# A two-block mixer network: the modulation's weights loaded as tiles of four k blocks, and its column-packed products issued in fours

## The chip, the cores and the metric

The kernel runs on one core of one Trainium2 chip. The metric is the device time of one execution in microseconds; lower is better. TensorE (PE) does the matrix products, VectorE (DVE), ScalarE (ACT) and GpSimd (POOL) the elementwise work, and SyncE (SP) issues nearly all loads, in the order of its queue. Each engine works through its own instructions strictly in program order.

## The reference, cut to what matters

Two blocks, each of two layers, work on 256 context and 256 latent tokens of 1024 features, all in float32. Each layer begins with a modulation: a vector `c` (one for the latent tokens, one for the context) goes through silu and a large matrix, and its result is cut into shifts, scales and gates.

```python
def first_block(x, c, ctx, c_ctx, ada_w, ada_b, ...):
    s_lat = jax.nn.silu(c)
    s_ctx = jax.nn.silu(c_ctx)
    for i in range(DEPTH):                      # DEPTH = 2, ada_w[i] is 1024 x 6144
        m_l = jnp.split((s_lat @ ada_w[i] + ada_b[i])[:, None, :], 6, axis=-1)
        m_c = jnp.split(s_ctx @ ada_w[i] + ada_b[i], 6, axis=-1)
        ul = snake(modulate(hl, m_l[0], m_l[1]))
        ...                                     # i = 0: GLA mixer, i = 1: SSD mixer
        hl = layer_norm(DEEPNORM_ALPHA * hl + m_l[2] * snake(yl), ...)
        hl = layer_norm(DEEPNORM_ALPHA * hl + m_l[5] * sq_relu_mlp(modulate(hl, m_l[3], m_l[4]), ...), ...)
...
def second_block(x, c, ctx, c_ctx, norm_g, w_ada, b_ada, w_in, ...):
    for l in range(DEPTH):                      # w_ada[l] is 1024 x 3072
        shift, scale, gate = jnp.split(jax.nn.silu(c) @ w_ada[l] + b_ada[l], 3, axis=-1)
        shift_c, scale_c, gate_c = jnp.split(jax.nn.silu(c_ctx) @ w_ada[l] + b_ada[l], 3, axis=-1)
        ...                                     # three attentions, gated and merged
```

The change touches only how `silu(c) @ ada_w` and `silu(c) @ w_ada` are computed.

## The kernel before, in words

**The program** runs through stages, with approximate times of the profile: the modulation of the first layer that must be there first (0 to 31 us), the GLA mixer (31 to 345), its output projection and norm (345 to 450), the first feed-forward net, called ffn0 (450 to 835), the SSD mixer (835 to 1190), its end and the start of the next stage (1190 to 1290), then the second feed-forward net, and from 1620 us the second block. The large projections all go through `gemm` (products at L432): a weight unit of two k blocks (512 KB, tile `wr`, three buffers) is loaded by SP at L380, split into a high part `wh` by ACT (L385) and a low part `wl` by DVE or POOL (L390), two buffers each, and multiplied in three terms per k block.

**The modulation** is cut into chunks of 512 columns, each 1024 x 512 values, that is eight k blocks of 128 rows. The first four chunks are computed at once (`early`, tile `wst`). The other 32 wait in a background queue (`self.bg`): after each weight unit, `gemm` calls `tick`, which adds `self.rate` to an account and records further steps of the queue while the account is positive; a step says what it costs. `finish(n)` records steps until n chunks are left. So the background work is woven into the projections by a rate: `FRATE` in ffn0, `SRATE` in the SSD mixer, `GRATE` in the GLA mixer. After that a scheduler orders each engine's instructions by a simulated timeline, and `not_before` keeps a load from going ahead of the products recorded before it.

A chunk is one generator, `ada_chunk`. There are two kinds:

- **22 of the 32 background chunks have two vectors** (`c` and `c_ctx`). Their k blocks are loaded one by one (256 KB each, tile `wrd`, four buffers), and each is the moving operand of one float32 product with 32 stationary columns (L531): 512 columns stream through a quarter of PE's columns. Products g = 0..3 write to rows 32g of one bank, so each has its own quarter of the array. A chunk has eight such products. A float32 product shows as two records in the profile. The four rows of sums are then added by four small products with `sel` (L540), once per group of up to four chunks, after a copy by ACT (L537).
- **10 of the 32 have one vector.** DVE multiplies each k block by a column of the vector and sums over k (L556, then L558 seven times), and PE sums over the partitions by four products with `ones` (L566).

The yields are the costs told to `tick`: `PEY` = 4 for a chunk of the first kind; for the second 1 per k block, and 2 more.

## Time and profile before

| | us |
|---|---|
| median of three timed runs | 2635.37 |
| lowest and highest of them | 2631.38, 2638.84 |
| the profiled execution, from first to last instruction | 2640.2 |
| PE busy in it | 2532.2 (96%) |
| DVE busy | 1660.6 (63%) |
| ACT busy | 1214.7 (46%) |
| POOL busy | 363.9 (14%) |

For the profiled execution its span is the only time at hand; it is 4.8 us (0.2%) above the median of the timed runs. Busy time of PE is the union of its records; since products overlap in the pipeline, how long a product keeps the next one waiting is read from the distance between two starts, not from a record's length. "Idle before" is the time in which the engine had nothing in flight.

### The profile page before, as it was taken

Reading aid. Unit: us, or ns where it says so; the run is one execution under the profiler, and the core shown is the slowest. Engines: PE = TensorE matmul, PEld = TensorE weight load, DVE = VectorE, ACT = ScalarE, POOL = GpSimd, SP = SyncE. Lnnn points to the kernel's source line nnn. Section 1 sums busy time; section 2 is a strip of 40 time slices with the busy share of each in tenths; the row PEclk is TensorE's granted clock in tenths of the full one; section 3 lists DMA queues with packets and bytes.
Section 4 is the critical chain, followed back from the end, with each engine's and each line's share of the span. In section 5 each row is a group of like instructions: output and inputs, shape, how many; then the busy total and the mean of one; then the engine's idle time right before and its main releaser. Section 6 shows DMA issues by size and latency. Waiting matters only on the chain. (4 is left out here: it accounts for less than half of the span.)

```text
span 2640.2 us, 37049 instructions
## 1 busy us (share of the span) xinstructions
PE 2532.2 (96%) x14015; PEld 1949.7 (74%) x14015; DVE 1660.6 (63%) x3155; ACT 1214.7 (46%) x2365; POOL 363.9 (14%) x308
## 2 busy tenths in 40 slices
PE   7999988999999899999889989999999999999999
PEld 4777666558887776677678968777777877887777
DVE  3455568325465865768785677686745557688766
ACT  3344534323323544545455545554535335555554
POOL 0011112100000222424330030100012001100010
PEclk8999988999999899999989999999999999999999
DMA  6222334555444443433555554221222335333245
GB/s 249 93 76 76 126 128 152 164 161 178 152 163 160 152 151 128 140 121 120 172 189 189 184 182 128 65 81 56 65 80 72 109 120 176 120 100 104 81 141 170
DMA packets 123827, 348.03 MB, mean 132 GB/s; under 512 B 16248, under 2 KB 22336, under 8 KB 123648
## 3 DMA queue, kind: packets, MB, share of 16 engines
q1 hardware_dynamic: 118736, 333.22, 39.0%
q0 software_dynamic: 3616, 12.06, 1.3%
q8 instruction: 110, 1.80, 0.3%
q14 instruction: 69, 0.57, 0.1%
q10 hardware_dynamic: 1296, 0.38, 0.1%
HBM read 338.75 MB, written 6.85 MB: 131 GB/s over the span
## 5 line engine op out<-in xcount | busy, mean ns | idle before, releaser
L385 ACT CAST wh<-wr 128x1024 fp32r<-128x1024 f32 (+3 forms) x461 | 471.7, 1024 | 744.3 <-PE acc L432 666.5
L390 DVE TENSOR_TENSOR wl<-wr,wh 128x1024 fp32r<-128x1024 f32 (+3 forms) x421 | 514.6, 1222 | 467.9 <-ACT wh L385 451.0
L432 PE MATMUL acc<-wl,xh 128*128 128x512 f32 (+3 forms) x1876 | 732.6, 392 | 27.5 <-DVE wl L390 14.3
L432 PE MATMUL acc<-wh,xl 128*128 128x512 f32 (+3 forms) x1876 | 721.9, 388 | 0.0
L432 PE MATMUL acc<-wh,xh 128*128 128x512 f32 (+3 forms) x1876 | 683.7, 392 | 13.2 <-ACT wh L385 6.8
L432 PEld LDWEIGHTS acc<-wl,xh 128*128 128x128 f32 x1876 | 358.8, 191 | 119.6 <-DVE wl L390 23.1
L432 PEld LDWEIGHTS acc<-wh,xh 128*128 128x128 f32 x1876 | 353.4, 191 | 103.3 <-issue 14.8
L432 PEld LDWEIGHTS acc<-wh,xl 128*128 128x128 f32 x1876 | 357.9, 191 | 83.0 <-issue 16.5
L432 PE MATMUL acc<-xl,wh 128*128 128x512 f32 (+2 forms) x1024 | 354.1, 348 | 7.7 <-DVE xl L690 7.7
L432 PE MATMUL acc<-xh,wh 128*128 128x512 f32 (+2 forms) x1024 | 356.2, 352 | 1.3 <-DVE scv L1143 1.3
L432 PE MATMUL acc<-xh,wl 128*128 128x512 f32 (+2 forms) x1024 | 339.4, 350 | 2.2 <-DVE wl L390 1.7
L432 PEld LDWEIGHTS acc<-xh,wh 128*128 128x128 f32 (+1 forms) x1024 | 195.9, 192 | 47.5 <-issue 17.1
L432 PEld LDWEIGHTS acc<-xl,wh 128*128 128x128 f32 (+1 forms) x1024 | 197.1, 192 | 39.2 <-issue 8.5
L432 PEld LDWEIGHTS acc<-xh,wl 128*128 128x128 f32 (+1 forms) x1024 | 194.2, 193 | 42.6 <-issue 14.0
L390 POOL TENSOR_TENSOR wl<-wr,wh 128x1024 fp32r<-128x1024 f32 x40 | 97.4, 2438 | 805.0 <-ACT wh L385 775.5
L1673 ACT ACTIVATE bP<-ps,bnm 128x512 f32<-128x512 f32 (+1 forms) x144 | 88.8, 623 | 84.5 <-DVE bnm L1670 61.6
L531 PE MATMUL aps<-wrd,s 128*32 128x512 f32 x256 | 109.0, 612 | 2.5 <-DMA wrd<-in_ada 2.5
L1670 DVE TENSOR_REDUCE bnm<-ps 128x1 f32<-128x512 f32 (+1 forms) x120 | 80.9, 685 | 32.9 <-PE ps L1660 32.6
L1143 DVE SCALAR_TENSOR_TENSOR scv<-acc,scw,scv 128x510 f32<-128x510 f32 (+3 forms) x140 | 86.2, 633 | 24.1 <-ACT scv L1139 23.4
L1908 POOL TENSOR_SCALAR bP<-bP,brc 128x512 f32<-128x512 f32 (+1 forms) x24 | 34.9, 1456 | 478.6 <-DVE brc L1905 453.2
L1564 ACT COPY bPT<-ps 128x512 f32<-128x512 f32 x75 | 43.2, 589 | 56.2 <-PE ps L1684 52.7
L558 DVE SCALAR_TENSOR_TENSOR adac<-wrd,s,adac 128x512 f32<-128x512 f32 x70 | 55.8, 797 | 16.9 <-DMA wrd<-in_ada 16.1
(423 smaller groups left out, 3255.5 us busy)
## 6 DMA issues: line engine op xcount, KB each, us to landing
wr<-in_w SPq DMA_DIRECT2D x136, 512.0 KB, 3.5
wr<-in_win SPq DMA_DIRECT2D x136, 512.0 KB, 3.6
wrd<-in_ada SPq DMA_DIRECT2D x256, 256.0 KB, 3.9
wr<-in_swin SPq DMA_DIRECT2D x52, 512.0 KB, 3.8
wr<-in_gwin SPq DMA_DIRECT2D x24, 512.0 KB, 3.4
wr<-in_wbr SPq DMA_DIRECT2D x24, 512.0 KB, 3.6
wr<-in_wout SPq DMA_DIRECT2D x24, 512.0 KB, 3.6
wst<-in_ada SPq DMA_DIRECT2D x16, 512.0 KB, 5.7
```

What stands on the lines that cost most here:

```text
L385: nc.scalar.copy(out=hi[:, :n], in_=raw[:, :n])
L390: getattr(nc, eng).tensor_tensor(out=lo[:, :n], in0=raw[:, :n], in1=hi[:, :n].bitcast(F32), op=ALU.subtract)
L432: mm = nc.tensor.matmul(out=o, lhsT=wv if kind == "F" else xv, rhs=xv if kind == "F" else wv, start=b["first"], stop=fin and b["left"] == 0)
L531: nc.tensor.matmul(out=p[32 * g:32 * g + 32, :], lhsT=s[:, half * 4 + g, 6 - 2 * i:38 - 2 * i], rhs=raw[g], start=first and half == 0, sto ...
L558: nc.vector.scalar_tensor_tensor(out=a, in0=x, scalar=c, in1=a, op0=ALU.mult, op1=ALU.add)
L1143: nc.vector.scalar_tensor_tensor(out=c[:, :, o0:o1], in0=pv[:, :, i0:i1], scalar=w[:, tap:tap + 1], in1=c[:, :, o0:o1], op0=ALU.mult, op1= ...
L1564: self.nc.scalar.copy(out=out, in_=in_)
L1670: nc.vector.tensor_reduce(out=nm[:, :n], in_=p.rearrange("p (n k) -> p n k", n=n), axis=AX.X, op=ALU.max, negate=True)
L1673: nc.scalar.activation(out=e[:, i * nk:(i + 1) * nk], in_=p[:, i * nk:(i + 1) * nk], func=AF.Exp, bias=nm[:, i:i + 1], accum_out=sm[i])
L1908: nc.gpsimd.tensor_scalar(out=b, in0=b, scalar1=rc[:, 1, i:i + 1], scalar2=None, op0=ALU.mult)
```

## The change

**One tile of four k blocks.** A half chunk is one tile of 128 x 2048 values, filled by two loads of 512 KB. The early chunks have 7 such buffers in place of 14 half as large; the background (`wrd`) has one in place of four quarter tiles, so it takes the same memory.

**Four products in a row.** The four products of a half follow one another, and the first of them is made to wait for the second of the two loads, so that none waits between them.

**No chunk is left to DVE.** All 32 background chunks take the first path. The ten of one vector form groups of up to four with their neighbours, so that 14 sums with `sel` replace 11 sums with `sel` and 10 with `ones`.

**Rates.** `FRATE` falls from 1.8 to 1.0 per weight unit, since each chunk now costs 4.

At the end of the SSD mixer the residual is loaded into the quarters of the one `wrd` tile. All comments and docstrings are taken out as well, which moves line numbers: L531 becomes L523, L540 L536, L432 L429, L516 L515, L380 L377.

```diff
-FRATE = (1.8, 1)
+FRATE = (1.0, 1)
...
-ONESET = 1
...
-SDELAY = 1
...
     def ada_chunk(self, w, ch, s, bt, dst, plus, early, group):
...
-        def load(i):
...
-            if early:
-                x = self.t([P, 1024], "wst", 14)
-                nc.sync.dma_start(out=x, in_=src)
-                return [x[:, :512], x[:, 512:]]
-            x = [self.ta([P, 512], "wrd", 4) for _ in range(2)]
+        for half in range(2):
+            x = self.t([P, 2048], "wst", 7) if early else self.ta([P, 2048], "wrd", 1)
             for j in range(2):
-                self.not_before(getattr(nc, WRENG).dma_start(out=x[j], in_=src[:, j * 512:(j + 1) * 512]))
-            return x
-        b = bt[:, ch * 4:ch * 4 + 4]
-        if early or len(dst) > ONESET:
...
-                for g in range(4):
-                    nc.tensor.matmul(out=p[32 * g:32 * g + 32, :], lhsT=s[:, half * 4 + g, 6 - 2 * i:38 - 2 * i], rhs=raw[g],
-                                     start=first and half == 0, stop=i == n - 1 and half == 1)
...
+                o = off + (2 * half + j) * P * 1024
+                src = w[o:o + P * 1024].rearrange("(p f) -> p f", p=P)
+                d = nc.sync.dma_start(out=x[:, j * 1024:(j + 1) * 1024], in_=src)
+                if not early:
+                    self.not_before(d)
...
+            for g in range(4):
+                mms.append(nc.tensor.matmul(
+                    out=p[32 * g:32 * g + 32, :], lhsT=s[:, half * 4 + g, 6 - 2 * i:38 - 2 * i],
+                    rhs=x[:, g * 512:(g + 1) * 512], start=first and half == 0, stop=i == n - 1 and half == 1))
+
+            self.tc.add_manual_dep(mms[0].ins, d.ins.name, mybir.DependencyInfo(
+                mybir.DependencyClass.Sync, mybir.DependencyReason.DATA), reason="starts with the others")
...
-        acc = [self.ta([P, 512], "adac", 2) for _ in dst]
-        for k in range(KD):
...
-                    nc.vector.scalar_tensor_tensor(out=a, in0=x, scalar=c, in1=a, op0=ALU.mult, op1=ALU.add)
-            yield len(dst)
...
     def block1(self, mode="r3", upto=99):
...
+            if m in (2, 4):
+                grp = self.group(4)
             am[1, m] = self.ada(ada[1], m, s, bt[1], sets, "am1", float(m in (1, 4)), False, grp)
...
+            hw = self.ta([P, 2048], "wrd", 1)
...
-                    x = self.ta([P, 512], "wrd", 4)
+                    x = hw[:, (2 * c + t) * 512:(2 * c + t + 1) * 512]
```

What stands where on the engines shows at three places. PE in ffn0, before, around two products of one chunk (`aps` is their bank, `wrd` the loaded k block; `acc`, `wh`, `wl`, `xh`, `xl` belong to the projection):

```order
L432 MATMUL acc_4608<-xh_3629,wh_4611 128x512
L531 MATMUL aps_4427<-wrd_4516,s_89 32x512
L432 MATMUL acc_4608<-xl_3630,wh_4611 128x512
L432 MATMUL acc_4608<-xh_3629,wl_4612 128x512
L531 MATMUL aps_4427<-wrd_4517,s_89 32x512
L432 MATMUL acc_4605<-xl_3634,wh_4641 128x512
```

The same place on PE in the changed kernel, at one half of a chunk in ffn0; 29 products of the projection follow before the other half's four:

```order
L429 MATMUL acc_5307<-wl_5387,xh_4960 128x512
L429 MATMUL acc_5307<-wh_5386,xl_4961 128x512
L523 MATMUL aps_5372<-wrd_5369,s_89 32x512 x4
L429 MATMUL acc_5308<-wl_5387,xh_4958 128x512
L429 MATMUL acc_5308<-wh_5386,xl_4959 128x512
```

Products that stood one by one between the projection's now stand four in a row, at half as many places or fewer. PE in the GLA mixer of the changed kernel, ahead of the second half's four of one chunk (`gkx`, `gv` are keys and values, `glah`, `glal` decays, `gm` a mask):

```order
L429 MATMUL acc_1017<-xh_133,wl_1075 128x512
L429 MATMUL acc_1017<-xh_135,wh_1074 128x512
L429 MATMUL acc_1017<-xl_136,wh_1074 128x512
L429 MATMUL acc_1017<-xh_135,wl_1075 128x512
L876 MATMUL ps_736<-gv_473,gkx_734 128x256
L876 MATMUL ps_742<-gv_473,gkx_740 128x256
L876 MATMUL ps_748<-gv_473,gkx_746 128x256
L896 MATMUL ps_753<-gm_68_375,glah_433 128x512
L896 MATMUL ps_753<-gm_68_375,glal_434 128x512
L896 MATMUL ps_757<-gm_68_375,glah_433 128x512
L896 MATMUL ps_757<-gm_68_375,glal_434 128x512
L523 MATMUL acc_1051<-wrd_1056,s_89 32x512 x4
```

The first half's four (`wrd_1048`) stand one product above the first row, so that twelve products lie between the two fours, and in that time the one `wrd` tile is loaded anew. SP's queue in the changed kernel at the two halves in ffn0:

```order
L515 DMA wrd_5369<-in_ada 128x1024 x2
L377 DMA wr_5482<-in_w 128x1024
L377 DMA wr_5526<-in_w 128x1024
L515 DMA wrd_5377<-in_ada 128x1024 x2
L377 DMA wr_5556<-in_w 128x1024
```

The second `wrd` load stands behind two loads of the projection's weights, and waits for the four products that read the tile before. Over the whole program PE has 12 halves in fours in the GLA mixer, 30 in ffn0 and 22 in the SSD mixer; three of the last 22 are cut into one product and three with a few others between.

## Rows read from the trace of the kernel before

**Rows 1.** The page: busy time, share of the span, instructions.

```profile
span 2640.2 us, 37049 instructions
PE 2532.2 (96%) x14015; PEld 1949.7 (74%) x14015; DVE 1660.6 (63%) x3155; ACT 1214.7 (46%) x2365; POOL 363.9 (14%) x308
```

**Rows 2.** Stretches: length, busy PE, PEld, DVE, ACT, POOL (records), clock, DMA share, GB/s.

```profile
31.00:345.00 314.00, 304.38 (x2449) 221.04 (x2450) 160.12 (x346) 147.99 (x273) 40.86 (x65) 0.97 0.30 97
581.00:835.00 254.00, 254.00 (x1132) 206.33 (x1131) 134.51 (x188) 86.00 (x123) 0.00 (x0) 1.00 0.49 163
905.00:1165.00 260.00, 255.13 (x1289) 174.86 (x1289) 171.27 (x322) 122.82 (x279) 79.59 (x58) 0.99 0.42 138
1190.00:1240.00 50.00, 45.46 (x248) 38.08 (x246) 40.54 (x74) 28.04 (x66) 21.28 (x15) 0.97 0.30 98
1190.00:1290.00 100.00, 89.20 (x479) 73.61 (x477) 88.82 (x146) 57.16 (x133) 47.67 (x35) 0.98 0.44 144
```

**Rows 3.** Waits of PE (total us, times, longest): 450 to 835, then 1190 to 1290.

```profile
PE acc L432 <- DVE xl L690: 1.1, 1, 1.1
...
PE acc L432 <- DVE scv L1143: 5.1, 3, 2.1
```

**Rows 4.** PE in order of time: start, length, line, names; one modulation product.

```profile
456.53 0.28 PE L432 MATMUL acc<-xl,wh 128*128 128x256 f32 x1
456.65 0.28 PE L432 MATMUL acc<-xh,wl 128*128 128x256 f32 x1
456.86 1.04 PE L531 MATMUL aps<-wrd,s 128*32 128x512 f32 x2
457.84 0.39 PE L432 MATMUL acc<-xh,wh 128*128 128x256 f32 x1
```

**Rows 5.** PE in order of time: four modulation products that met, at two places.

```profile
500.89 0.40 PE L432 MATMUL acc<-xh,wl 128*128 128x512 f32 x1
501.13 0.39 PE L432 MATMUL acc<-xh,wh 128*128 128x512 f32 x1
501.46 1.07 PE L531 MATMUL aps<-wrd,s 128*32 128x512 f32 x8
502.45 0.50 PE L432 MATMUL acc<-xl,wh 128*128 128x512 f32 x1
...
176.85 1.03 PE L905 MATMUL ps<-gv,gkx 128*128 128x256 f32 x4
177.80 1.06 PE L531 MATMUL acc<-wrd,s 128*32 128x512 f32 x8
```

**Rows 6.** The same table for L531's products on PE alone.

```profile
0.00:31.00 31.00, 17.59 (x64) 0.98 0.96 365
31.00:345.00 314.00, 30.15 (x96) 0.97 0.30 97
450.00:835.00 385.00, 46.03 (x96) 1.00 0.50 165
835.00:1190.00 355.00, 62.93 (x160) 0.97 0.43 141
```

**Rows 7.** Groups from 450 to 835: count, busy us, mean ns, idle before.

```profile
L566 PE MATMUL aps<-ones,adac 128*128 128x1 f32 x64 | 7.6, 239 | 0.0
L540 PE MATMUL aps<-sel,adac 128*128 128x4 f32 (+1 forms) x16 | 1.9, 244 | 0.0
```

**Rows 8.** The stretch table for L558's operations on DVE alone.

```profile
1190.00:1290.00 100.00, 13.07 (x13) 0.98 0.44 144
```

**Rows 9.** The page: loads by line, KB each, us to landing.

```profile
wr<-in_w SPq DMA_DIRECT2D x136, 512.0 KB, 3.5
wst<-in_ada SPq DMA_DIRECT2D x16, 512.0 KB, 5.7
```

**Rows 10.** The stretch table again, of all engines, at the start.

```profile
5.00:10.00 5.00, 4.92 (x16) 0.74 (x16) 0.00 (x0) 0.00 (x0) 0.00 (x0) 1.00 1.04 408
32.00:36.00 4.00, 2.50 (x10) 1.35 (x8) 3.41 (x9) 3.56 (x8) 0.00 (x0) 0.50 0.31 118
```

More of the change, by code (lines that the diff above doesn't have):

```diff
@@ L518, in ada_chunk @@
-        b = bt[:, ch * 4:ch * 4 + 4]
-        if early or len(dst) > ONESET:
-            tag = ("ps", 3) if early else self.bgtag
-            first, n = group["p"] is None, group["n"]
-            i = len(group["dst"])
-            group["dst"].append((dst, b, plus))
-            for half in range(2):
-                raw = load(2 * half) + load(2 * half + 1)
-                if group["p"] is None:
-                    group["p"] = self.ps(*tag)
-                p = group["p"]
-                for g in range(4):
-                    nc.tensor.matmul(out=p[32 * g:32 * g + 32, :], lhsT=s[:, half * 4 + g, 6 - 2 * i:38 - 2 * i], rhs=raw[g],
-                                     start=first and half == 0, stop=i == n - 1 and half == 1)
-            if i < n - 1:
-                yield PEY
-                return
-            r = self.ta([P, 512], "adac", 2)
-            nc.scalar.copy(out=r, in_=p)
-            p = self.ps(*tag)
-            for j in range(4):
-                nc.tensor.matmul(out=p[:, 2 * n * j:2 * n * j + 2 * n], lhsT=r[:, j * P:(j + 1) * P], rhs=self.sel[:, :2 * n],
-                                 start=j == 0, stop=j == 3)
-            for i, (dst, b, plus) in enumerate(group["dst"]):
-                for si, d in dst:
-                    nc.vector.scalar_tensor_tensor(out=d, in0=p[:, 0:8 * n].rearrange("p (j s) -> p s j", j=4)[:, 2 * i + si, :],
-                                                   scalar=plus, in1=b, op0=ALU.add, op1=ALU.add)
@@ new lines, in ada_chunk @@
+        b = bt[:, ch * 4:ch * 4 + 4]
+        tag = ("ps", 3) if early else self.bgtag
+        first, n = group["p"] is None, group["n"]
+        i = len(group["dst"])
+        group["dst"].append((dst, b, plus))
+        for half in range(2):
+            x = self.t([P, 2048], "wst", 7) if early else self.ta([P, 2048], "wrd", 1)
+            for j in range(2):
+                o = off + (2 * half + j) * P * 1024
[3 more added lines that the diff above has]
+                    self.not_before(d)
+            if group["p"] is None:
+                group["p"] = self.ps(*tag)
+            p = group["p"]
+            mms = []
+            for g in range(4):
[4 more added lines that the diff above has]
+                mybir.DependencyClass.Sync, mybir.DependencyReason.DATA), reason="starts with the others")
@@ L546, in ada_chunk @@
+        if i < n - 1:
             yield PEY
             return
-        acc = [self.ta([P, 512], "adac", 2) for _ in dst]
-        for k in range(KD):
-            if k % 2 == 0:
-                raw = load(k // 2)
-            x = raw[k % 2]
-            for a, (si, _) in zip(acc, dst):
-                c = s[:, k, 6 + si:7 + si]
-                if k == 0:
-                    nc.vector.tensor_scalar(out=a, in0=x, scalar1=c, scalar2=None, op0=ALU.mult)
-                else:
-                    nc.vector.scalar_tensor_tensor(out=a, in0=x, scalar=c, in1=a, op0=ALU.mult, op1=ALU.add)
-            yield len(dst)
@@ L560, in ada_chunk @@
-        for _ in range(SDELAY):
-            yield 2
-        p = self.ps(*self.bgtag)
-        for n, a in enumerate(acc):
-            for j in range(4):
-                mm = nc.tensor.matmul(out=p[:, n * 4 + j:n * 4 + j + 1], lhsT=a[:, j * P:(j + 1) * P],
-                                      rhs=self.ones[:, :1], start=True, stop=True)
-                if n == j == 0:
-                    self.not_before(mm)
-        for n, (_, d) in enumerate(dst):
-            nc.vector.scalar_tensor_tensor(out=d, in0=p[:, n * 4:n * 4 + 4], scalar=plus, in1=b, op0=ALU.add, op1=ALU.add)
+        r = self.ta([P, 512], "adac", 2)
@@ new lines, in ada_chunk @@
+        nc.scalar.copy(out=r, in_=p)
+        p = self.ps(*tag)
+        for j in range(4):
+            nc.tensor.matmul(out=p[:, 2 * n * j:2 * n * j + 2 * n], lhsT=r[:, j * P:(j + 1) * P], rhs=self.sel[:, :2 * n],
+                             start=j == 0, stop=j == 3)
+        for i, (dst, b, plus) in enumerate(group["dst"]):
+            for si, d in dst:
+                nc.vector.scalar_tensor_tensor(out=d, in0=p[:, 0:8 * n].rearrange("p (j s) -> p s j", j=4)[:, 2 * i + si, :],
+                                               scalar=plus, in1=b, op0=ALU.add, op1=ALU.add)
```

3 lines of the change are left out of this document (1 added, 2 removed).

## The prediction

> **What bounds the kernel now.** I read the page first: PE is busy in 96% of the span, DVE in 63%, the others in less [rows 1]. A share over the whole span hides stages, so the table by stretch came next. From 581 to 835 us, most of ffn0, PE is busy in all of 254.00 us; in the GLA mixer in 304.38 of 314, in the heart of the SSD mixer in 255.13 of 260 [rows 2]. The waits of PE say the same: in the whole of ffn0 it waited 1.1 us [rows 3]. So in every stretch that has background work PE is what the others wait for, and the question is how much of PE's time the change frees, and who is next.
>
> A modulation product alone shows what it costs. The projection's product before it starts at 456.65, the one after it at 457.84; two ordinary ones there are 0.12 apart (456.53, 456.65), so one modulation product holds up the stream by 1.19 - 0.12 = 1.07 us [rows 4]. Where four of them happened to meet (eight records, two for each product), the neighbours start at 501.13 and 502.45, and ordinary ones are 0.24 apart: 1.08 us for all four [rows 5]. Four products in different quarters of the array run side by side, one alone takes as long as four. That is what the change uses.
>
> **Term 1, the products in fours.** L531 outside the start is busy 30.15 us in the GLA mixer, 46.03 in ffn0 and 62.93 in the SSD mixer, 139.1 in all for 352 records, that is 176 products [rows 6]. A stretch of it, with one product or four, lasts 1.04 to 1.07 [rows 4, 5]; at 1.05 these are 132 stretches, so most products stood alone. They cost 132.5 x 1.07 = 141.8 us of PE's stream: 30.7 in the GLA mixer, 46.9 in ffn0, 64.1 in the SSD mixer. The changed kernel has 64 halves (12, 30 and 22), of which three are cut in two: 67 stretches of 1.08 = 72.4 us, though it has ten chunks more on PE. Net: -17.7 in the GLA mixer, -14.5 in ffn0, -37.1 in the SSD mixer, **-69.4 us**.
>
> The Trainium skill's page "TensorE: Matmul & The Clock Gate" (section "Part 3: Packing small matmuls — row/col tiling") lists smaller speedups than four, 3.07 for four row tiles and 2.38 for three column tiles. By 3.07 a stretch of four would cost 1.07 x 4 / 3.07 = 1.39 us, 67 of them 93 us, and the net would be -49. Here the row decides, since it is the same product in the same place.
>
> **Term 2, the sums.** Eight sums with `ones` take 7.6 us in ffn0, two with `sel` 1.9, so 0.95 for either kind [rows 7]. Ten of the first go, three of the second come (14 for 11): **-6.6 us** of PE, -5.7 of it in ffn0 (eight go, two come).
>
> **Term 3, DVE.** 80 operations leave DVE, 64 of them in ffn0. There PE waited 1.1 us for DVE in all [rows 3], so they give nothing. Of the rest, 13 with 13.07 us lie between 1190 and 1290 [rows 8], where DVE is busy 88.82 of 100 us [rows 2] and PE waited 5.1 us for its convolution [rows 3]. Between nothing and -5 I take **-3**.
>
> **Term 4, the single buffer.** Now the second half's load waits, in SP's queue, for the first half's four, and the second four wait for the load. The projection's products behind them on PE wait too. Two loads of 512 KB have to land. One alone took 3.5 us in ffn0, one in the saturated start 5.7 [rows 9]. With the second issued some 0.4 later, the pair needs between 3.9 and 6.1; at the start 408 GB/s were moved [rows 10], at which 512 KB are 1.3 us, so my estimate is 3.5 + 1.3 = 4.8 us. Against it stands the work that PE has between the two fours. In ffn0 that is 29 products x 0.24 = 7.0 us at the place shown, and 6.8 to 10 over all fifteen chunks: hidden even at 6.1, and I keep 1 us for a collision with the projection's loads (0 to 4). In the SSD mixer ten of eleven chunks have 6 to 10 us and one 2.4: **+3** (2 to 5). In the GLA mixer the twelve products shown are nine of 512 columns and three of 256: 9 x 0.24 + 3 x 0.47 = 3.6 us, where 0.47 is half of the 0.95 between 176.85 and 177.80 [rows 5]. Summed like this, nine reloads there have 3 to 6 us, 4.4 on average, since `finish` puts three chunks at the end: +6 at a reload of 4.8, +14 at 6.1, and as the first three pairs have a projection's load between them I take **+10**. The loads queued behind on SP (gate rows, `wr`) wait with them; in ffn0 the two `wr` loads ahead of the second half's are due before the first four run, so they hold nothing up.
>
> **Term 5, what is late next.** Freed time is worth its length only while PE stays the last to arrive. In ffn0 DVE will be less busy than before, so there it is. In the SSD mixer the nearest row without PE's background work is 1190 to 1240: PE idle 9% (45.46 of 50 busy) against 2% from 905 to 1165 [rows 2]. If that stretch went from 255.1 us of PE work to 217 and to 9% idle, it would take 239, not 222: 17 us given back. DVE had its own chunk in that comparison row, which it loses now, so I take **+9** (0 to 17).
>
> **Term 6, the start.** The eight early fours need about 8.6 us of PE where L531 had 17.59 [rows 6], but the 16 loads of 512 KB take 20.6 us at 408 GB/s [rows 10] either way: nothing is won. PE was granted its full clock (1.00, which is 2.4 GHz) while it was busy 4.92 of 5 us, and half of it (0.50, 1.2 GHz) from 32 to 36 us after a looser stretch [rows 10]. With less to do it may be at half from the first loads on. What would then be slower is the last four (+1), the sums and the first transposes: **+2** (0 to 4).
>
> **The sum.** -69.4 - 6.6 - 3 + (1 + 3 + 10) + 9 + 2 = -54 us. The span is 2640.2 us and the median of the timed runs 2635.4; I take the difference from the median: **2581 us**. With every term at its good end it is -73, 2562; at its bad end -32, 2603.
>
> **The rivals.**
> - *The background products were filler.* In the GLA and SSD mixers chains of DVE, ACT and POOL set the pace, and the products ran while PE would have waited. Then only ffn0 gains (14.5 + 5.7, less 3 for the reload and the start): -17, 2618 us. For it speaks the 9% idle of 1190 to 1240; against it that from 905 to 1165 PE idles 2% while DVE is at 171 of 260.
> - *The single buffer becomes the bound, and the kernel is slower.* The place is the second four of each chunk. If a reload takes 10 us, by loads that queue behind the projection's, the waits are 9 x 5.6 in the GLA mixer, 15 x 2 in ffn0 and 11 x 2 in the SSD mixer, 102 us in place of 14: +34, 2669 us. It decides from a reload of about 9 us on, where the waits have eaten the gain; the rows have 3.5 to 5.7 for one load. The Trainium skill asks for the opposite of this edit: "Double-buffer for performance: Overlap DMA with compute" ("Trainium Kernel Development and Optimization", Best Practices). This trace before has four buffers and hardly a wait on them, so it can't tell.
> - *Fours pay only 3.07-fold,* as on the page above: 67 stretches of 1.39 us where I have 1.08 add 21: 2602 us. Both places in the trace with four speak against it.
> - *The change doesn't do what it says:* the four run one after the other, 1.08 + 3 x 0.98 = 4.0 us (0.98 from 456.86 to 457.84 [rows 4]), and 64 of them cost 256 us instead of 142: some 2750. The order has them in a row, and the trace shows such rows at 1.08, so this is close to ruled out.
>
> **How the numbers follow.** Forecast 0.77 (2562 to 2603), filler 0.11, single buffer 0.07, fours at 3.07 0.04, not as it says 0.01. The range takes the forecast's own ends, a little beyond them below, and reaches above towards the filler case: 2558 to 2612. About 0.3%, 8 us, is what a measurement can tell from no change: faster than 2627 are the forecast, nearly all of the filler case and the fours at 3.07, 0.88; slower than 2643 the single buffer and the last, 0.07; in between, where filler and some waiting meet, 0.05.
>
> **What the profile after would show.** L523 with 256 background products in 512 records, stretches of x8 at about 1.07, and about 70 us busy against 139.1. ffn0 shorter by some 19 us with PE still at 100%. Waits of PE on `wrd` loads: about 10 us in the GLA mixer, next to none in ffn0; tens of us there would mean the second rival. In the SSD mixer more idle before the projection's and the conv's products; if the stage doesn't shrink by 20 us or more, the filler rival holds. `aps<-ones` and DVE's `adac<-wrd` are gone. The second block should take what it took; its instruction order differs in places by the scheduler alone, and a shift of more than 5 us there is outside my terms.

## The result and the profile after

The changed kernel takes 2555.75 us (median of four runs, 2553.72 to 2563.77) where the kernel before, measured beside it, takes 2637.11 (four runs, 2631.38 to 2649.83): a ratio of 0.969, 95% interval 0.966 to 0.972. It is faster by 81 us. Forecast were 2581 us and a range from 2558 to 2612, so the direction came out, and the time lies 25 us below the forecast and 2 us below the range. The profiled execution has a span of 2562.0 us against 2640.2, a difference of 78.2; sums over stages are made against that one.

The page of the changed kernel, which answers to [rows 1] and [rows 9]:

```profile
span 2562.0 us, 36991 instructions
PE 2449.3 (96%) x14119; PEld 1936.6 (76%) x14119; DVE 1603.4 (63%) x3075; ACT 1214.1 (47%) x2368; POOL 357.9 (14%) x308
...
wrd<-in_ada SPq DMA_DIRECT2D x128, 512.0 KB, 4.4
...
wst<-in_ada SPq DMA_DIRECT2D x16, 512.0 KB, 7.1
```

PE's share is the same 96%: it lost 82.9 us of busy time and the span lost 78.2. This is the first sign that nearly all of PE's freed time was saved and almost nothing given back as idle time.

One four in ffn0, PE in order of time (start, length, line, names), which answers to [rows 4] and [rows 5]; then L523's products by stretch (length, busy PE with records, clock, DMA share, GB/s), which answers to [rows 6]:

```profile
546.62 0.40 PE L429 MATMUL acc<-xh,wl 128*128 128x512 f32 x1
546.94 1.07 PE L523 MATMUL aps<-wrd,s 128*32 128x512 f32 x8
547.94 0.50 PE L429 MATMUL acc<-xh,wh 128*128 128x512 f32 x1
```

```profile
31.00:345.00 314.00, 12.85 (x96) 0.95 0.28 94
440.00:800.00 360.00, 30.91 (x232) 1.00 0.51 174
800.00:1155.00 355.00, 28.46 (x184) 0.97 0.46 159
```

The neighbours of the four start 1.32 us apart, as they did where four had met by chance, and outside the start L523 is busy 72.2 us for 512 records where L531 was busy 139.1 for 352.

To see where the time went I cut both traces at the same four products of the large projections (the 701st, 2301st, 3601st and 3801st record of `gemm` in order of time) and put every stretch from one PE start to the next on the instruction that began it, idle time apart. A "place" is a run of modulation products without other work in it. The first of the four cuts lies within the output projection of the GLA mixer, so the row ffn0 holds the end of that projection and the norm as well.

| stage | before: length, us | modulation (places) | sums | other work | idle | after: length, us | modulation (places) | sums | other work | idle |
|---|---|---|---|---|---|---|---|---|---|---|
| GLA mixer and output | 364.0 | 27.7 (29) | 4.9 | 313.8 | 17.7 | 345.2 | 12.0 (12) | 5.8 | 311.1 | 16.3 |
| ffn0 | 430.4 | 43.0 (44) | 7.3 | 370.6 | 9.5 | 413.9 | 28.9 (29) | 3.2 | 368.7 | 13.1 |
| SSD mixer | 411.0 | 59.0 (59) | 3.2 | 328.6 | 20.1 | 369.2 | 26.7 (26) | 3.2 | 322.1 | 17.2 |
| its end | 71.3 | 0 | 1.6 | 62.6 | 7.1 | 68.4 | 0 | 0 | 61.5 | 6.9 |

The start is 2.7 us longer (36.5 to 39.2), everything behind the table's end 1.1 shorter. The change is thus +2.7 of start, -62.1 of modulation products, -4.8 of sums, -12.2 of other work (with it the step into and out of a place, which is paid at half as many places, and some clock), -0.9 of idle time and -1.1 of the rest: -78.4, which is the spans' difference of 78.2 up to rounding. The stages as rows of the stretch table, before first, then after (length, busy PE, PEld, DVE, ACT, POOL with records, clock, DMA share, GB/s), which answers to [rows 2]:

```profile
36.50:400.50 364.00, 346.31 (x2904) 253.14 (x2903) 190.08 (x402) 163.59 (x300) 50.15 (x80) 0.95 0.31 102
400.50:830.90 430.40, 420.86 (x1820) 308.93 (x1819) 216.21 (x317) 149.44 (x235) 30.85 (x12) 0.98 0.50 163
830.90:1241.80 410.90, 390.87 (x2018) 287.96 (x2016) 287.23 (x547) 196.59 (x428) 121.36 (x85) 0.97 0.41 136
```

```profile
39.20:384.50 345.30, 328.96 (x2903) 248.58 (x2902) 192.96 (x406) 162.20 (x299) 50.28 (x80) 0.97 0.31 107
384.50:798.40 413.90, 400.80 (x1916) 304.03 (x1915) 172.19 (x249) 150.72 (x238) 30.75 (x12) 0.98 0.51 171
798.40:1167.60 369.20, 351.99 (x2043) 284.60 (x2042) 276.41 (x539) 195.51 (x426) 124.71 (x90) 0.97 0.46 159
```

In the SSD mixer PE's busy time fell by 38.9 us and the stage by 41.7: idle time did not rise. That is where the forecast had set aside 9 us.

**The single buffer** is seen in the waits of PE, which answers to [rows 3]. The kernel before, 31 to 400 us (total us, times, longest); then the changed one, 31 to 385 and 798 to 1168:

```profile
PE ps L995 <- DVE go L988: 7.3, 2, 3.9
```

```profile
PE acc L523 <- DMA wrd<-in_ada: 5.1, 6, 1.6
...
PE ps L966 <- DVE go L959: 0.4, 2, 0.2
...
PE aps L523 <- DMA wrd<-in_ada: 1.0, 1, 1.0
```

Six waits for the reload have come, 5.1 us in the GLA mixer, one of 1.0 in the SSD mixer, none in ffn0. In PE's order of time (the last bracket is idle time and its releaser) they look like this:

```profile
315.43 1.13 PE L876 MATMUL ps<-gv,gkx 128*128 128x256 f32 x4
...
321.45 1.07 PE L523 MATMUL acc<-wrd,s 128*32 128x512 f32 x8 [0.70 <-DMA wrd<-in_ada]
322.45 0.50 PE L896 MATMUL ps<-gm,xh 128*128 128x512 f32 x1
...
327.42 1.07 PE L523 MATMUL acc<-wrd,s 128*32 128x512 f32 x8 [1.47 <-DMA wrd<-in_ada]
```

From the end of one four to the start of the next (315.43 to 321.45, 322.45 to 327.42) a reload took 6.0 and 5.0 us, at or above the 4.8 of the forecast.

Yet the stage's idle time fell, from 17.7 to 16.3, because another wait went: the 7.3 us for `go`, the normed output of a head, are down to 0.4. PE there, before and then after:

```profile
379.98 0.67 PE L977 MATMUL ps<-gv,gAT 128*128 128x256 f32 x2 [1.41 <-DVE gAT L972]
384.56 1.97 PE L995 MATMUL ps<-ident,go 128*128 128x128 f32 x8 [3.91 <-DVE go L988]
```

```profile
361.14 0.60 PE L948 MATMUL ps<-gv,gAT 128*128 128x256 f32 x2
362.44 0.73 PE L429 MATMUL acc<-wh,xh 128*128 128x512 f32 x2 [0.70 <-ACT wh L382]
...
366.48 0.44 PE L966 MATMUL ps<-ident,go 128*128 128x128 f32 x2 [0.21 <-DVE go L959]
```

Before, nothing stood between the last head's products and the transposes of `go`. Now a dozen products of the output projection do, and 21 more just ahead of the last head's. Before, the projection had used up what it could by 374 us, and PE stood idle for the last head.

The products are left over because the projection's weights come later. SP's queue, before and after (start, length, line, names):

```profile
275.51 11.07 SPq L516 DMA_DIRECT2D wrd<-in_ada  x8
...
288.69 26.51 SPq L516 DMA_DIRECT2D wrd<-in_ada  x16
...
334.79 42.12 SPq L380 DMA_DIRECT2D wr<-in_gwout  x6
```

```profile
295.87 0.88 SPq L515 DMA_DIRECT2D wrd<-in_ada  x2
...
308.49 27.03 SPq L515 DMA_DIRECT2D wrd<-in_ada  x10
...
354.61 9.39 SPq L377 DMA_DIRECT2D wr<-in_gwout  x3
```

The projection's sixth load, the first behind these, is issued 66 us ahead of the stage's end before, 30 after. The single buffer does not explain that. The rows are the same three chunks, 24 loads of 256 KB before and 12 of 512 KB after, and they take the queue equally long: 39.7 us (275.51 to 315.20) and 39.7 (295.87 to 335.52). After, they begin 20 us later, in both kernels directly behind the projection's fourth load. Between the last of them and the sixth load, SP waits mostly for the gate row that ACT copies out once the last chunk is summed (11.7 us before, 11.2 after) and for a free weight buffer (6.0 and 4.0), and not for the tile. Why the scheduler's order has all of this later stays open.

### The profile page after: what moved, and what is told of

Same layout as the page of the kernel before. It is cut to its first block, busy times and chain, and to the rows that moved or that the text cites. A ratio compares the mean times of both kernels' runs of the same rounds, so it can differ in the third digit from the quotient of the medians.

```text
span 2562.0 us, 36991 instructions
## 1 busy us (share of the span) xinstructions
PE 2449.3 (96%) x14119; PEld 1936.6 (76%) x14119; DVE 1603.4 (63%) x3075; ACT 1214.1 (47%) x2368; POOL 357.9 (14%) x308
## 5 line engine op out<-in xcount | busy, mean ns | idle before, releaser
L429 PE MATMUL acc<-wl,xh 128*128 128x512 f32 (+3 forms) x1876 | 731.5, 391 | 26.1 <-DVE wl L387 14.7
L429 PE MATMUL acc<-wh,xl 128*128 128x512 f32 (+3 forms) x1876 | 722.5, 388 | 0.0
L429 PE MATMUL acc<-wh,xh 128*128 128x512 f32 (+3 forms) x1876 | 680.4, 391 | 10.5 <-ACT wh L382 4.7
L429 PEld LDWEIGHTS acc<-wl,xh 128*128 128x128 f32 x1876 | 358.9, 191 | 115.6 <-DVE wl L387 23.8
L429 PEld LDWEIGHTS acc<-wh,xh 128*128 128x128 f32 x1876 | 352.6, 191 | 93.9 <-issue 12.4
L429 PEld LDWEIGHTS acc<-wh,xl 128*128 128x128 f32 x1876 | 358.4, 191 | 72.3 <-issue 5.8
L429 PE MATMUL acc<-xl,wh 128*128 128x512 f32 (+2 forms) x1024 | 354.2, 348 | 11.6 <-DVE xl L661 11.6
L429 PE MATMUL acc<-xh,wh 128*128 128x512 f32 (+2 forms) x1024 | 355.1, 351 | 2.1 <-ACT wh L382 1.2
L429 PE MATMUL acc<-xh,wl 128*128 128x512 f32 (+2 forms) x1024 | 340.3, 349 | 0.6 <-POOL wl L387 0.6
L429 PEld LDWEIGHTS acc<-xl,wh 128*128 128x128 f32 (+1 forms) x1024 | 196.9, 192 | 42.0 <-DVE xl L661 12.8
L429 PEld LDWEIGHTS acc<-xh,wh 128*128 128x128 f32 (+1 forms) x1024 | 195.8, 192 | 40.8 <-issue 9.4
L429 PEld LDWEIGHTS acc<-xh,wl 128*128 128x128 f32 (+1 forms) x1024 | 194.4, 193 | 28.5 <-issue 3.5
L523 PE MATMUL aps<-wrd,s 128*32 128x512 f32 x416 | 59.4, 607 | 1.1 <-DMA wrd<-in_ada 1.0
L1658 PE MATMUL ps<-ident,bP 128*128 128x128 f32 x400 | 60.2, 276 | 0.0
```

Source lines behind the costliest of these rows:

```text
L429: mm = nc.tensor.matmul(out=o, lhsT=wv if kind == "F" else xv, rhs=xv if kind == "F" else wv, start=b["first"], stop=fin and b["left"] == 0)
L523: mms.append(nc.tensor.matmul(out=p[32 * g:32 * g + 32, :], lhsT=s[:, half * 4 + g, 6 - 2 * i:38 - 2 * i], rhs=x[:, g * 512:(g + 1) * 512] ...
L1658: nc.tensor.transpose(p[:, d:d + P], e[:, c:c + P], self.ident)
```

## The experiments

Each ratio is against runs of the kernel before that were measured beside it; stage lengths are of each kernel's profiled execution, cut as above. "Places" are those of all three stages.

**The changed kernel once more,** as the measure for those compared with it.

> The changed kernel as it is, beside the three below on the same chip, as their measure. Both theories: 0.969 of the kernel before, 2554 us where the kernel before takes 2636.

Measured: 2556.72 us, 0.967 (0.965 to 0.970). Its span is 2554.4, 7.6 below the other profiled execution of the same code: 3.4 of it in the GLA mixer and 3.2 behind the table's end. So a difference of some 4 us in one stage of two profiled executions tells nothing. The idle times repeat more closely (14.5, 13.0, 16.9 and 7.1 us in the four stages).

**What pays: places, or tile, loads and engine?** Three kernels change one thing each. The first takes the kernel before and gives the ten one-vector chunks to PE as well, everything in single products:

```diff
-FRATE = (1.8, 1)
+FRATE = (1.0, 1)
-ONESET = 1
+ONESET = 0
...
+            if m in (2, 4):
+                grp = self.group(4)
```

> All 32 background chunks go to PE, but product by product from quarter tiles as before (256 products, none in a row), rate 1.0, groups as in the changed kernel. 'Stretches': 256 x 1.07 = 274 us where before had 142, sums -6.6: +125 us at most, ratio 1.047. 'DVE relief': the SSD mixer and the stretch after it get faster by 10 to 20 us of it, ratio 1.04. 'Filler' (the products in the GLA and SSD mixers ran while PE would have waited): only ffn0 pays, 120 - 47 - 6 = +67, ratio 1.025.

Measured: 2725.47 us, 1.032 (1.029 to 1.036). ffn0 grew to 512.4 us with 116 places, the SSD mixer to 417.1 with 74. Not all products stood alone: there are 219 places and not 256, 87 more than in the kernel before. ffn0 paid 82.0 us for 72 of them, the SSD mixer 6.1 us for 15, as its idle time fell from 20.1 to 13.3 us. So the measured +85 us (by the ratio) lie between the sums of the theory of stretches and of the filler rival, and this run alone does not decide between them; nor does it tell whether DVE's relief or the order filled the idle time. PE there, in order of time:

```profile
562.75 0.40 PE L432 MATMUL acc<-wh,xl 128*128 128x512 f32 x1
563.09 1.04 PE L531 MATMUL aps<-wrd,s 128*32 128x512 f32 x2
564.06 0.51 PE L432 MATMUL acc<-wh,xh 128*128 128x512 f32 x1
```

From neighbour to neighbour (562.75 to 564.06) a single product takes 1.31 us; a four takes 1.32.

The second is the changed kernel with two tiles of two k blocks in place of one of four, so the loads stay at 512 KB, but only two products follow one another:

```diff
-        for half in range(2):
-            x = self.t([P, 2048], "wst", 7) if early else self.ta([P, 2048], "wrd", 1)
...
+        for q in range(2 if early else 4):
...
+                x = self.ta([P, 1024], "wrd", 2)
...
```

> As the changed kernel, but a background tile is two k blocks (one load of 512 KB, two buffers), and products are issued two in a row: 130 stretches for 260 products. Loads are as large and as many as in the changed kernel. 'Stretches': 130 x 1.07 = 139 us where before had 142, sums -6.6: about -10 us, ratio 0.996. Rival 'larger loads' (the gain is that 128 loads of 512 KB take the place of 256 of 256 KB): most of the gain stays, ratio 0.975 or less.

Measured: 2633.79 us over ten runs, 0.999 (0.997 to 1.001), with 126 places where the kernel before has 132. The larger loads, the larger tile and the chunks taken from DVE are all in it, and it is not faster.

The third is the changed kernel without the wait of a four's first product for both loads (the two lines with `add_manual_dep` are out). It leaves the scheduler free, which then puts mostly pairs.

> The changed kernel without the wait of the first of the four for the second load. Tiles and loads are unchanged; the scheduler now puts the products of the first load ahead, 110 pairs, 7 single, few threes and fours, 125 stretches. 'Stretches': 134 us where before had 142, sums -6.6: -14 us, ratio 0.995. Rival 'the tile does it': ratio within 0.3% of the changed kernel's 0.969.

Measured: 2614.54 us, 0.991 (0.988 to 0.994), 128 places. Of the 19 us that it gains on the pairs with two tiles 10.4 are in the GLA mixer (346.0 against 356.4 us), where it has 11.6 us of idle time against 15.4 and 306.1 of other work against 315.2; the runs on the rate, below, come back to that.

So the number of places decides first: 219 give a span of 2723.6 us, 132 give 2640.2, 126 and 128 give 2632.6 and 2613.6, 67 give 2562.0 and 2554.4. From 219 down to 67 that is 1.1 us for a place.

**Fours for the two-vector chunks alone.** The one-vector chunks go back to DVE, reading the same tile of four k blocks:

```diff
-FRATE = (1.0, 1)
+FRATE = (1.8, 1)
...
+        if not early and len(dst) == 1:
+            acc = self.ta([P, 512], "adac", 2)
...
+                    nc.vector.scalar_tensor_tensor(out=acc, in0=xk, scalar=c, in1=acc, op0=ALU.mult, op1=ALU.add)
+                yield 1
+            yield 2
...
+            return
...
-            if m in (2, 4):
-                grp = self.group(4)
```

> The four-in-a-row tiles are kept for the chunks of two vectors (43 fours, 2 pairs); the ten chunks of one vector stay with DVE, at the old rate of 1.8. Theory 'stretches' (PE is the last to arrive everywhere, each stretch of modulation products costs 1.07 us of PE whether it holds one product or four): 47 stretches cost 50 us where before had 142, the sums stay: -92 us, ratio 0.965, some 10 us faster than the changed kernel. Rival 'DVE relief' (the SSD mixer gained more than its products because DVE lost its chunks): not faster than the changed kernel, ratio 0.969 or more.

Measured: 2553.45 us, 0.967 (0.964 to 0.970), not to be told from the changed kernel, where the theory of stretches had it some 10 us faster. It has 45 places. Its profiled execution is the shortest of its four (2548.89 us). The stretch table for ffn0 and the SSD mixer, to be held against the rows of the changed kernel above:

```profile
378.40:779.90 401.50, 386.29 (x1820) 307.62 (x1819) 214.17 (x313) 150.30 (x236) 29.71 (x12) 0.97 0.51 175
779.90:1148.70 368.80, 346.96 (x2018) 283.41 (x2017) 285.48 (x545) 195.18 (x424) 120.27 (x83) 0.97 0.44 150
```

ffn0 is 12.4 us shorter with DVE at 214.17 of 401.50 us: there the sums cost DVE time that nobody waits for, and PE is spared 17 places. In the SSD mixer PE is 5.0 us less busy and the stage as long as the changed kernel's, with 21.8 us of idle time against 17.2, and its end is 3.2 us longer (71.6). So the second part of the change, the ten chunks, is worth nothing that the times can tell; it costs time in ffn0, and what it gives in the SSD mixer and its end is smaller than one profiled execution can show. The gain of the whole change is the fours'.

**Is PE the bound in each stage?** Each background four of the changed kernel is issued twice:

```diff
-            for g in range(4):
+            for g in [0, 1, 2, 3] * (1 if early else 2):
...
```

> The changed kernel with each background four issued twice: the modulation's sums come out wrong, all else is as it was. 64 fours more. Theory 'TensorE's stream is the bound in every stage': each costs its 0.98 to 1.07 us, +63 to +69 us, 12 in the GLA mixer, 30 in ffn0, 22 in the SSD mixer; 0.994. Rival 'filler' (in the mixers they run while TensorE would wait): only ffn0 pays, +30 to +35 us, 0.982. In between, the share that each stage pays is the share of its freed time that the change could keep.

Measured: 2616.15 us, 0.990 (0.987 to 0.993), 60 us above the changed kernel by the ratios and 62.4 by the spans. By stage against the changed kernel run beside it: GLA mixer +10.0 for 12 fours, ffn0 +23.5 for 29, SSD mixer +23.9 for 23 (by the cuts above; the section on the change counts one of these to ffn0, 30 and 22), and PE's idle time hardly moved (13.4, 11.6 and 19.6 us). The mixers pay as ffn0 does, 0.8 to 1.0 us for a four. The filler rival is out: by the table the mixers also shrank, by 18.8 and 41.8 us.

```profile
485.70 0.40 PE L429 MATMUL acc<-wh,xh 128*128 128x512 f32 x1
486.03 1.92 PE L523 MATMUL aps<-wrd,s 128*32 128x512 f32 x16
487.88 0.50 PE L429 MATMUL acc<-wl,xh 128*128 128x512 f32 x1
488.22 0.39 PE L429 MATMUL acc<-wh,xl 128*128 128x512 f32 x1
```

PE in order of time shows a doubled four: 1.85 us from its start to the next one's, against 1.00 for one. The second adds 0.85. The products next to the place start 0.33 and 0.34 us apart from it or from their next, where ordinary ones are 0.24 apart [rows 5].

**How far does freed time stay freed?** The second half of each background chunk is left out, loads and products, so that half of each modulation sum is missing:

```diff
-        for half in range(2):
+        for half in range(2 if early else 1):
...
```

> The changed kernel with the second half of every background chunk left out, its loads and its four products: 32 fours and 32 pairs of loads fewer, and half of each modulation sum is missing from the result. No wait on the tile is left within a chunk. Theory 'TensorE's stream is still the bound': -32 x 1.07 = -34 us (GLA mixer -6, ffn0 -16, SSD mixer -12), 0.954 to 0.956. Rival 'filler, from here on' (the idle time of the mixers rises as their background gets thin): ffn0 alone, -16 to -20, 0.960 or more.

Measured: 2531.08 us, 0.958 (0.956 to 0.960), some 25 us below the changed kernel where PE's stream alone would give 34. ffn0 gave its 16.9 us and the SSD mixer 13.4. The GLA mixer grew by 8.4. Its row, and the waits of PE in it:

```profile
38.80:389.00 350.20, 329.29 (x2854) 255.38 (x2853) 188.09 (x401) 161.60 (x299) 46.41 (x80) 0.93 0.26 88
```

```profile
PE ps L966 <- DVE go L959: 9.4, 3, 3.9
```

Idle time there is 20.9 us against 14.5, the granted clock 0.93 against 0.97. In the GLA mixer taking out half of the changed kernel's fours gave nothing; in the SSD mixer it gave 13.4 us for 12 of them, about their length.

**Does the reload cost what PE waits for it?** Three runs. In the first the second half of a chunk uses the first half's tile again; the second half's loads are left out, and eight products stand in a row:

```diff
-            x = self.t([P, 2048], "wst", 7) if early else self.ta([P, 2048], "wrd", 1)
-            for j in range(2):
+            if early or half == 0:
+                x = self.t([P, 2048], "wst", 7) if early else self.ta([P, 2048], "wrd", 1)
+            for j in range(2 if early or half == 0 else 0):
```

> The changed kernel, except that the second half of each background chunk uses the first half's tile again: half of the modulation's weight loads (of the background) are left out, and the output is computed with wrong weights. There is nothing to wait for between the halves, so the eight products stand in a row. Theory 'the reload costs what TensorE is seen to wait': the 5 + 1 us of waits on the tile go, and with one entry per chunk where there were two some 32 x 0.1 us more, so 5 to 10 us faster than the changed kernel, 0.966. Rival 'the reload binds more than the waits show' (by the 14 us of the forecast or more, through the loads behind it in the queue): 15 us faster or more, 0.963 or less.

Measured: 2561.55 us, 0.969 (0.965 to 0.973): no gain by the median, though the waits on the tile are down to 0.7 us in all. Its four executions lie far apart, from 2547.78 to 2568.76 us, and the profiled one is the longest, so its rows tell only why that one is long. ffn0 is 4.6 us shorter there, but the GLA mixer is 15.9 longer: 57 us of it at half the clock against 17, and 8.5 us of waits for `go`:

```profile
PE ps L967 <- DVE go L960: 8.5, 3, 3.9
```

```profile
215.00:237.00 22.00, 22.00 (x172) 14.80 (x171) 8.08 (x17) 13.15 (x21) 2.94 (x5) 0.62 0.10 31
```

The other two only change the rate of the background in the heads of the GLA mixer, and so the places of the fours; the first spreads them, the second leaves more for the stage's end:

```diff
-GRATE = (0, 0.6, 0.6, 0.6)
+GRATE = (0, 1.2, 1.2, 1.2)
```

> The changed kernel with one number changed: in the GLA mixer's second and third head the background runs at 1.2 of the work, not 0.6, so the fours of its last chunks don't wait for the stage's end and stand farther apart. Theory 'waits on the reload are what the close fours cost' : the 5 us of TensorE's waits on the tile in the GLA mixer go to 1 or none, 3 to 5 us faster than the changed kernel, 0.966. Rival 'the wait only takes the place of another' (what TensorE didn't wait for the tile, it waits for the gates' chain): the idle time of the stage stays at 14 to 16 us, 0.967 to 0.969.

```diff
-GRATE = (0, 0.6, 0.6, 0.6)
+GRATE = (0, 0.3, 0.3, 0.3)
```

> The changed kernel with the background of the GLA mixer at 0.3 of the work in its second to fourth head, not 0.6: more chunks are left for the stage's end, and their halves stand close together. Theory 'the waits on the tile cost their length': two or three more chunks with 1 to 1.6 us of wait for each, the GLA mixer 2 to 5 us longer, 0.970. Rival 'the wait stands where TensorE would have waited for the gate chain anyway': waits on the tile rise, the idle time of the stage stays within 1.5 us of the changed kernel's 14.5 to 16.3, 0.968.

Measured: 2573.10 us, 0.974 (0.971 to 0.977), and 2574.19, 0.974 (0.972 to 0.976): both some 12 to 18 us slower than the changed kernel by the ratios, 6 to 10 of them in the GLA mixer (352.0 and 351.3 us, where the two profiles of the changed kernel have 345.2 and 341.8). Waits of PE in the GLA mixer at 1.2:

```profile
PE ps L966 <- DVE go L959: 7.3, 2, 3.9
PE acc L523 <- DMA wrd<-in_ada: 3.3, 3, 2.2
```

At 0.3 I had expected more waits on the tile, and there are next to none there (0.2 us); the premise fell, not only the number. But at 1.2 the waits on the tile stand beside the old 7.3 us for `go`, and idle time in the GLA mixer is 21.9 us, where the kernel before had 17.7 with the same 7.3: it fits waits on the tile that cost about their length, though the two kernels differ in more than these waits. Both rates also moved half a chunk from ffn0 to the SSD mixer (28 fours and 24, where the changed kernel has 29 and 23), which with its end is 5.6 and 3.3 us longer.

What sorts all fifteen profiles (the kernel before, the changed one, the thirteen experiments) is the output projection's sixth load:

| sixth load ahead of the GLA stage's end, us | kernels | waits for `go`, us | idle, us | stage without modulation and sums, us |
|---|---|---|---|---|
| 27 to 33 | changed (both), DVE's chunks, no common wait, doubled fours, early pairs | 0.2 to 1.8 | 11.6 to 16.3 | 317.7 to 327.4 |
| 48 to 77 | before, single products, pairs, tile used twice, halves, rates 1.2 (three) and 0.3 | 3.9 to 9.4 | 15.4 to 24.1 | 326.9 to 335.4 |

The means of the last column are 323 and 332 us, though the two ranges touch (327.4 and 326.9). So some 9 us of the GLA mixer, waits and clock together, go with an order in which the projection's products are left over for the last head; between the kernel before (331.4) and the two profiles of the changed one (327.4 and 324.6) it is 4 to 7. That the late load makes the difference is an inference: no run moved that load alone. Nor is the single buffer shown to make the load late: all six kernels of the first group have it, but so have six of the nine of the second.

**The early chunks in pairs again,** in fourteen tiles of two k blocks as before:

```diff
-        for half in range(2):
-            x = self.t([P, 2048], "wst", 7) if early else self.ta([P, 2048], "wrd", 1)
+        for q in range(4 if early else 2):
+            m = 1 if early else 2
+            x = self.t([P, 1024], "wst", 14) if early else self.ta([P, 2048], "wrd", 1)
...
```

> The changed kernel with the two early chunks loaded as before, two k blocks to a tile of which there are fourteen. Theory 'clock at the start' (the coarser loads let TensorE run dry, the granted clock falls to half sooner, and that is the 2.7 us by which the first projection starts later): the start gets back 2 to 3 us, 0.968. Rival (the later start is what the later order of the loads costs, or chance): within 0.5 us of the changed kernel, 0.969.

Measured: 2564.37 us, 0.971 (0.968 to 0.974). The start gave back 2.2 us (36.6 against 38.8), the size that the theory had. Stretches of the start, 25 to 31 us: the kernel before, the changed one, the changed one once more, this one:

```profile
25.00:31.00 6.00, 4.44 (x24) 2.38 (x22) 2.04 (x12) 2.33 (x6) 0.00 (x0) 0.88 1.03 406
```

```profile
25.00:31.00 6.00, 4.33 (x19) 2.62 (x20) 0.48 (x7) 0.58 (x1) 0.00 (x0) 0.57 1.03 406
```

```profile
25.00:31.00 6.00, 4.15 (x25) 2.72 (x26) 1.18 (x9) 1.15 (x2) 0.00 (x0) 0.81 1.03 406
```

```profile
25.00:31.00 6.00, 4.66 (x24) 2.46 (x22) 1.93 (x12) 2.22 (x5) 0.00 (x0) 0.81 1.03 406
```

But the clock is not the reason, or only a small part of it. In the first profile of the changed kernel it is at half from 25.9 us on, in the second from 28.8, and with pairs from 28.7. The second has the clock of the pairs in this stretch, 0.81, and its first projection still starts at 38.8 us; the first, with 0.57, starts it at 39.2. So the early fall goes with 0.4 us, and the other 2.2 belong to the coarser tiles in another way. With fours DVE is busy 0.48 and 1.18 us in the stretch, with pairs 2.04 and 1.93, so the work behind the sums comes later; which step holds it up is not shown. And the whole is some 8 us longer than the changed kernel: +3.5 in ffn0 (3.0 of it idle time), +2.1 in the SSD mixer's end, +2.4 behind it. No instruction of those stages was changed, only the order that the scheduler found. This stays unexplained.

**Two candidates:** fours for the two-vector chunks with the rate at 1.2 in the GLA mixer, once with the early pairs as well (the diffs above put together).

> Candidate: the changed kernel with the one-vector chunks summed by VectorE as before, the early chunks in pairs as before, and the background at 1.2 in the GLA mixer. By the earlier runs: start -2.2, GLA mixer -3, ffn0 -12 (in the profile of the run with VectorE's chunks), the other stages as they are: 2545, 0.963. Rival (the ends of the stages are set by VectorE's and ScalarE's chains, which the ten chunks lengthen): 2553, 0.967.

> The same without the early pairs: the one-vector chunks summed by VectorE, the background at 1.2 in the GLA mixer. By the earlier runs 2548, 0.964; rival as for the one before, 2553, 0.967.

Measured: 2565.53 us, 0.971 (0.968 to 0.973), and 2563.15, 0.970 (0.967 to 0.973). Both have the short ffn0 (398.8 and 397.9 us) and lose it in the GLA mixer (352.5 and 351.2, idle 21.3 and 24.1) and at the SSD mixer's end (81.0 and 82.9). It is the rate that fails them: the second differs from the run with DVE's chunks (0.967) by the rate alone. No version was found that can be told from the changed kernel on the good side.

## Why the forecast was short

**The bound was read rightly.** PE's share, the 2% of idle time in the mixers and the price of a place from two neighbours' starts said that PE's stream is the time. The doubled fours confirm it stage by stage. For work taken out, the halves confirm it in ffn0 and the SSD mixer, and not in the GLA mixer.

**Terms 1 and 2 together were right.** The forecast had -76.0 of PE's work; measured are -62.1 and -4.8, and -12.2 of other work. The places were counted well: 132 and 67 in the sum, 132 and 67 in the traces. The 12.2 belong here: the product ahead of a place and the one behind it take some 0.1 us more each (in ffn0 of the changed kernel 0.33 and 0.34 us over 27 places, where ordinary ones take 0.23), 65 places x 0.2 = 13 us, of which my 1.07 us for a place held one half. Fours cost what one cost: four take 1.32 us from neighbour to neighbour and one takes 1.31, which is four-fold. The Trainium skill's page "TensorE: Matmul & The Clock Gate" (section "Part 3: Packing small matmuls — row/col tiling") lists 3.07 for four row tiles. These are four column tiles, and the traces do not show that figure for them.

**Term 3 came out in size, by luck.** The SSD mixer's end is 2.9 us shorter, 3 were forecast, as less waiting for DVE's convolution. But 1.6 of the 2.9 are sums that Term 2 had counted, and idle time fell by 0.2. PE's waits for `scv`, over the SSD mixer and its end 5.6 us before, are still 4.6:

```profile
PE acc L429 <- DVE scv L1114: 4.6, 2, 3.7
```

The run with DVE's chunks put back has the end 3.2 us longer, 1.6 of it sums and 1.6 idle time.

**Term 4 failed in size, and left out its other side:** +14 us for the single buffer, +10 of it in the GLA mixer. There were six waits with 5.1 us where nine with some 10 had been summed, 1.0 in the SSD mixer where I had 3, none in ffn0: 6 us. What the sum had no term for is the order: PE has products of the projection left where it had waited 7.3 us for `go`, and that wait went to 0.4. So the GLA mixer's idle time fell by 1.4 us where +10 was forecast. The wait for `go` was in the trace of before, but I had read the waits of ffn0 and of the SSD mixer's end alone. The fourth and the sixth of the projection's loads come later in this order, and why stays open; the waits on the tile do not show as its cause.

The Trainium skill's rule that I had quoted against this edit is "Double-buffer for performance: Overlap DMA with compute" ("Trainium Kernel Development and Optimization", Best Practices). The lone tile cost the 6 us of waits, and the pairs with two tiles of half the size are 3% slower than the fours with one, so the rule did not decide here. No run has two tiles of four k blocks, so what a second buffer would give the fours is not shown.

**Term 5 failed:** +9 us of idle time in the SSD mixer, measured are -2.9. It was taken from 1190 to 1240 as the nearest row without PE's background. That row is from the end of the stage, where DVE's own chunk ran and PE waited for `scv`; it tells nothing of the middle. PE's modulation work in this stage was 74.3, 59.0, 49.5, 44.2, 26.7 and 11.1 us in the single products, the kernel before, the doubled fours, the pairs, the changed kernel and the halves, and its idle time 13.3, 20.1, 19.6, 15.5, 17.2 and 19.8: it does not follow the background in this range.

**Term 6 came out in size, not by the clock:** +2 forecast, +2.7 and +2.3 measured, and 2.2 given back by pairs. The forecast had it from a clock at half from the first loads on. The two profiles of the changed kernel, with 0.57 and 0.81 from 25 to 31 us, put the clock's part at some 0.4 us; the rest is the coarser tiles' and unexplained, so the size was luck.

In sum the forecast is short by 24 us of the spans' 78.2. It had 20 us of added idle time (14 for the single buffer, 9 for the SSD mixer, less the 3 of Term 3), and measured are -0.9: -1.4 in the GLA mixer, +3.6 in ffn0, -2.9 in the SSD mixer, -0.2 at its end. That is 21 of the 24; the other 3 are PE's work, -79.1 where -76.0 was forecast. The range's lower end, 2558, rested on a sum of good ends (-73) with 8 us of waits in it and no gain beyond the work that PE loses; an order that changes can fill old waits, and the range had no room for that.

## What to carry to other kernels

Where four narrow products share the array, count the places at which the stream changes over, not the products; a wait that keeps four together was worth more here than the freedom to start each early (2614 us without it, 2556 with it, 0.991 and 0.969 of the kernel before). Price the idle time that a lighter stream may expose by adding or removing work in the stage itself, not by the idle share of a neighbouring row: doubled fours cost their length in all three stages, and halved ones gave nothing in one. And read the waits of every stage that the change reorders, also those that it seems not to touch: what moves into an old wait is a gain that no list of removed work holds.

## What the runs showed of the hardware

**Work behind a wait can run at half the clock, so that the wait costs more than its length.** In the kernel before, PE idles 3.39 and 3.91 us for `go` at the end of the GLA mixer (to 344.34 and to 384.56 us), and the clock is at half from 343.5 to 350.4 and from 381.1 to 391.3. The stretch around the first wait's end, and the one around the same transposes after:

```profile
343.00:351.00 8.00, 6.66 (x63) 5.31 (x64) 6.23 (x17) 2.54 (x5) 0.00 (x0) 0.57 0.00 0
```

```profile
324.00:332.00 8.00, 6.29 (x97) 4.33 (x87) 7.09 (x15) 3.15 (x7) 3.09 (x5) 1.00 0.57 212
```

The granted clock is 0.57 before, that is mostly at half (1.2 GHz), and 1.00 (2.4 GHz) after. The sixteen transposes behind the two waits (L995, then L966) show the price (count: duration ns min/median/max, first and last start, tiles):

```profile
L995 PE MATMUL ps<-ident,go x16: 415/421/476, 344.3 to 386.1; 128*128 128x128 f32 x16
```

```profile
L966 PE MATMUL ps<-ident,go x16: 270/272/329, 324.8 to 368.5; 128*128 128x128 f32 x16
```

Over the whole GLA mixer 33 us were at half clock before and 21 and 17 after. With the tile used twice it was 57, and there the stretch from 215 to 237 us, shown above, has PE busy in all of 22.00 us at a clock of 0.62. So a wait is not all that goes with half the clock, and being busy by the profile did not keep PE at full speed.
